# Products q, k, v and of the short convolution: weights as stationary operand, channels on partitions, no VectorE transposes

## The chip, the cores and the metric

The kernel runs on one core of one Trainium2 chip. The metric is the device time of one execution in microseconds (us). The median of three executions of the kernel before is 1896.12 us (1893.32 to 1897.59).

## The reference, cut to what matters

One decoder layer on 256 positions of 2048 channels: two mixers side by side (a gated delta rule, and a short gated convolution), gates, an output projection, and a SwiGLU network. All numbers are float32.

```python
xn = rms_norm(h, ln_mix_g[l])
proj = jnp.einsum('btd,de->bte', xn, w_in[l])
q, k, v, z, b, a, sc_b, sc_c, sc_h, gate_a, gate_b = partition(proj, IN_SIZES)
o_a = gdn_branch(q, k, v, z, b, a, conv_w, ...)   # depthwise conv over time (4 taps), silu,
                                                  # l2 norm of q and k, chunked delta rule
o_b = sc_b * causal_dwconv(sc_c * sc_h, conv_sc_w[l])          # 3 taps
merged = (sigmoid(gate_a) * (o_a @ w_proj_a) + sigmoid(gate_b) * (o_b @ w_proj_b))
h = h + merged @ w_out
hn = rms_norm(h, ln_ffn_g[l])
h = h + (silu(hn @ w_gate) * (hn @ w_up)) @ w_down
return rms_norm(h, ln_final_g)
```

The convolutions run along time, separately for each channel.

## The kernel before, in words

**Tiling.** Every projection is cut into products of 512 output channels. A product contracts 2048 channels in 16 k-tiles of 128 (5632 in 44 for the last one). Weights arrive by DMA in groups of two k-tiles (`raw`, 128x2x512), ScalarE rounds them to a high part (`wh`), VectorE subtracts to get the low part (`wl`), and TensorE makes three matmuls in place of one exact one: high by high, low by high, high by low. The same split of the normed input, with channels on partitions and time along the row, is `xg`; it stays resident for all products from `w_in`.

**Orientation.** In `product` (L383) the 128x128 stationary operand is a piece of the activations (128 channels by 128 positions), and the moving operand is 512 columns of weights. So the result has positions on partitions: two PSUM tiles (m = 0, 1: 128 positions each) of 512 channels, 2 x 3 x 16 = 96 matmuls of 512 columns per product.

**What follows a product.** The normalization factor of a position, `rx`, is a number per partition here, so ScalarE applies it as it moves the PSUM tile out (`evac_rows`, L504). The convolution wants channels on partitions and time along the row, so `flip` (L509) turns the 256x512 block with 16 transposes of 32x256 on VectorE. Then `conv` (L519) runs: ScalarE one tap, VectorE the others. `post_qk` and `post_v` do this for q, k, v of each of four groups of heads; `post_p` and `post_b` for the short convolution: sc_c, its product with sc_h, and sc_b. The products z, of the gates, of the projections and of the feed-forward network stay as they are and are not part of the change.

**Order of products.** Per group g: k, z of the group before, q, v; then four rounds of scc, sch, scb (after the first scc the last z). That is 28 products from the start to 724 us; 24 of them are touched (12 of k, q, v, 12 of scc, sch, scb). Each is 8 groups of weights.

**What sets the order around them.** Each engine runs its instructions in the order in which the program issues them. While `product` issues its matmuls it calls `step` after each k-tile: a planner (`Pace`) keeps an estimated clock per engine, and a follow-up task (a Python generator, one of `post_*`, `decay`, `core`) is advanced when its inputs are estimated to be ready by TensorE's clock. TensorE's small matmuls (the Gram matrices `gr`, sums of squares `ssb`, the triangular inverse `z`, `y`, the outputs `u`, `o`, transposes `vt`, `oc`) are thus dropped in between k-tiles. At most two products may hold PSUM banks (`MM` is 4 banks); before a product starts, `force` advances the most urgent task until one of them is evacuated, ready or not. A ticket (`turn`) lets the follow-ups of k, q, v, scc, scb run one after the other.

**PSUM.** The matmuls of product i+2 go to the banks of product i (in force cases: of product i+1), so they wait for its evacuation.

Of the kernel before, what the change touches and what calls it, by code (L numbers as in the profile page):

```python
# [9 lines left out]
F32 = mybir.dt.float32  # L10
# [5 lines left out]
P = 128  # L16
# [178 lines left out]
def tile_gdn_shortconv_layer(  # L195
# [184 lines left out]
        turn[1] += 1  # L380
        return turn[1] - 1

    def product(stat, KT, nm, after=None, stagger=None, guard=None):  # L383
        while len(pending) > MM // 2 - 1:
            force()
        pt = [ps_mm.tile([P, W], F32, tag="mm", name=f"mm{m}_{nm}") for m in range(2)]

        def terms(m, k, wh, wl):
            hi, lo = stat[k // HG]
            for e, (a, w) in enumerate(((hi, wh), (lo, wh), (hi, wl))):  # L390
                pe.matmul(
                    pt[m], a[:, k % HG, m * P:(m + 1) * P], w[:, k % KGRP, :],
                    start=(k == 0 and e == 0), stop=(k == KT - 1 and e == 2),
                )

        late = KT - KGRP * (AHEAD + 1) if stagger else KT
        kept = []
        for k0 in range(0, KT, KGRP):
            if guard is not None and k0 == KT - HG:
                drain(guard)  # L400
            i = nxt[1]
            nxt[1] += 1
            ensure(i)
            wh, wl = ready.pop(i)
            for k in range(k0, k0 + KGRP):
                for m in range(2):
                    if m == 0 or k < late:
                        terms(m, k, wh, wl)
                    else:
                        kept.append((m, k, wh, wl))  # L410
                if k < k0 + KGRP - 1:
                    step()
            if after is not None:
                after(k0 // KGRP)
            ensure(i + AHEAD + 1)
            step()
        pending.append(pt)
        if kept:
            stagger(pt)
            for t in kept:  # L420
                terms(*t)
        return pt
# [3 lines left out]
    nc.scalar.dma_start(g_mix, ln_mix)  # L426
    ident = gp.tile([P, P], F32, name="ident")
    make_identity(nc, ident)
    ones = gp.tile([P, P], F32, name="ones")
    nc.gpsimd.memset(ones, 1.0)  # L430
    upper = gp.tile([P, P], F32, name="upper")
    lower = gp.tile([P, P], F32, tag="rb", name="lower")
# [39 lines left out]
    def rsqrt(v, n, nm, scale):  # L472
# [17 lines left out]
            dve.scalar_tensor_tensor(out=y, in0=u, scalar=1.5, in1=y, op0=ALU.add, op1=ALU.mult)  # L490
        return y, t

    def bc(ap, n):
        return ap.unsqueeze(2).broadcast_to([P, ap.shape[1], n])

    def rows_tile(nm):
        return io.tile([P, 2, W], F32, tag="rows", name=nm)

    def chan_tile(nm):
        return io.tile([P, HG, T], F32, tag="cv", name=nm)  # L500
# [103 lines left out]
    def scalars():  # L604
# [6 lines left out]
        rx_, _ = rsqrt(ssx, 2, "x", 1.0 / D)  # L611
        dve.tensor_copy(rx, rx_)

    def scalars2():
        yield
        ba = small.tile([P, 2, 2 * H], F32, tag="ba", name="ba", bufs=1)
        bat = gp.tile([2 * H, T], F32, tag="tb", name="bat")
        act.copy(bat, pb[2 * H:])
        dve.tensor_tensor(bat, pb[:2 * H], bat, op=ALU.add)
        for i in range(0, P, SQ):  # L620
            dve.transpose(
                out=ba[i:i + SQ], in_=bat.rearrange("p (m t) -> p m t", t=P)[:, :, i:i + SQ]
            )
        for m in range(2):
            dve.tensor_scalar(
                out=ba[:, m, :], in0=ba[:, m, :], scalar1=rx[:, m:m + 1], scalar2=None, op0=ALU.mult
            )
        sx = small.tile([P, 2, H], F32, tag="spx", name="sp_x", bufs=1)
        dve.tensor_tensor(
            sx, ba[:, :, H:2 * H], dtb.unsqueeze(1).broadcast_to([P, 2, H]), op=ALU.add  # L630
        )
        sa = small.tile([P, 2, H], F32, tag="spa", name="sp_a", bufs=1)
        dve.scalar_tensor_tensor(
            out=sa, in0=sx, scalar=-1.0, in1=sx, op0=ALU.mult, op1=ALU.min
        )
# [14 lines left out]
        yield  # L650
        dve.tensor_copy(gdec_r[:, 0], gdec)
        dve.tensor_tensor(gdec_r[:, 1], gdec, gdec_r[:, 0], op=ALU.subtract)
        dve.tensor_copy(gdec_rf, gdec_r)
        yield 1
        b = bank("aj")
        pe.matmul(b[:, :H], lower, gdec[:, 0, :], start=True, stop=True)
        dve.tensor_copy(aj, b[:, :H])
        mark("gdec")


    def post_qk(g, qk, pt, me):
        while turn[0] < me - 1:
            yield
        nm = f"{'kq'[qk]}{g}"
        rows = rows_tile(f"rows_{nm}")
        evac_rows(pt, rows)
        yield
        if g:
            yield from need(("gram", g - 1))
# [7 lines left out]
        while turn[0] < me:  # L677
            yield
        off = H if qk == 0 else 0
        full = io.tile([P, HG, T], F32, tag="fc", name=f"fc_{nm}", bufs=1)  # L680
        yield from flip(rows, full)
        while turn[0] < me:
            yield
        y = chan_tile(f"cv_{nm}")
        yield from conv(
            full, lambda c, i: wc[:, off + HG * g + c, i:i + 1], 4, y, 0, y
# [47 lines left out]
    def post_v(g, pt, me):  # L734
        while turn[0] < me - 1:
            yield
        nm = f"v{g}"
        rows = rows_tile(f"rows_{nm}")
        evac_rows(pt, rows)
        yield  # L740
        while turn[0] < me:
            yield
        full = io.tile([P, HG, T], F32, tag="fc", name=f"fc_{nm}", bufs=1)
        yield from flip(rows, full)
        while turn[0] < me:
            yield
        y = chan_tile(f"cv_{nm}")
        yield from conv(full, lambda c, i: wc[:, 2 * H + HG * g + c, i:i + 1], 4, y, 0, y)
        turn[0] += 1
        yield  # L750
        yield from need(("sc", g))
        if g:
            yield from need(("done", g - 1))
        yield 2
        vs = st["sc", g][1]
        v = gp.tile([P, 2, HG, P], F32, tag="v", name=f"v_{g}")
        for m in range(2):
            b = bank(f"vt_{g}_{m}")
            for c in range(HG):
                pe.transpose(  # L760
                    b[:, c * P:(c + 1) * P], y[:, c, m * P:(m + 1) * P], ident
                )
            for c in range(HG):
                act.activation(
                    v[:, m, c, :], b[:, c * P:(c + 1) * P], AF.Copy, scale=vs[:, m, c:c + 1]
                )
        mark(("v", g), v)
# [279 lines left out]

    last = None
    for g in range(NG):
        pt = product(xg, KD, f"k{g}", after=None if g else after_first)  # L1050
        if g == 0:
            scalars()
            spawn(scalars2())
        spawn(post_qk(g, 0, pt, ticket()))
        spawn(decay(g))
        last = spawn(core(g))
        if g:
            product_z(g - 1)
        pt = product(xg, KD, f"q{g}")
        spawn(post_qk(g, 1, pt, ticket()))  # L1060
        pt = product(xg, KD, f"v{g}")
        spawn(post_v(g, pt, ticket()))


    ob = [None] * NS

    def post_p(n, pt, me):
        while turn[0] < me - 1:
            yield
        rows = rows_tile(f"scc{n}")  # L1070
        evac_rows(pt, rows)
        yield
        yield from need(("h", n))
        pt = st["h", n]
        for m in range(2):
            dve.scalar_tensor_tensor(
                out=rows[:, m, :], in0=pt[m], scalar=rx[:, m:m + 1], in1=rows[:, m, :],
                op0=ALU.mult, op1=ALU.mult,
            )
        close(pt)  # L1080
        yield
        while turn[0] < me:
            yield
        y = chan_tile(f"sy{n}")
        st["y", n] = y
        ch = io.tile([P, HG, T], F32, tag="fc", name=f"sf{n}", bufs=1)
        yield from flip(rows, ch)
        yield from conv(ch, lambda c, i: wsc[:, HG * n + c, i:i + 1], 3, y, SOON)
        turn[0] += 1

    def post_b(n, pt, me):
        while turn[0] < me - 1:
            yield
        if n == 1:
            yield from need(("oc", NG - 1))
            open_late()
        rows = rows_tile(f"scb{n}")
        evac_rows(pt, rows)
        yield
        while turn[0] < me:  # L1100
            yield
        y = st["y", n]
        ch = io.tile([P, HG, T], F32, tag="fc", name=f"bf{n}", bufs=1)
        yield from flip(rows, ch)
        both(y, y, ch, ALU.mult)
        yield SOON
        if n == 0:
# [10 lines left out]
        ob[1:] = [pair(lp, f"s{NS + i}", f"ob{i}") for i in (1, 2, 3)]  # L1118

    for n in range(NS):  # L1120
        pt = product(xg, KD, f"scc{n}")
        spawn(post_p(n, pt, ticket()))
        if n == 0:
            product_z(NG - 1)
        pt = product(xg, KD, f"sch{n}")
        pace.end = pace.t["pe"]
        mark(("h", n), pt)
        pt = product(xg, KD, f"scb{n}")
        lastb = spawn(post_b(n, pt, ticket()))


# [242 lines left out]
```

## Time and profile before

| | |
|---|---|
| median of 3 runs | 1896.12 us |
| the profiled execution's own time | 1895.74 us |
| its span, first to last instruction | 1893.7 us |
| TensorE busy | 1868.0 us, 99% |
| its weight loads (beside the matmuls) | 1538.5 us, 81% |
| VectorE busy | 1322.7 us, 70% |
| ScalarE busy | 954.0 us, 50% |
| mean granted TensorE clock | 0.996 |

PE is TensorE's matmuls, PEld its weight loads, DVE VectorE, ACT ScalarE. A matmul's duration in the profile (0.39 us for 512 columns) is longer than the distance to the next one's start, since matmuls are pipelined: what a matmul costs in a stream is the distance between starts. The stretch that the change touches ends at 724 us, where the first gate product starts.

### The profile page before, as it was taken

Reading aid. Unit: us, or ns where it says so; the run is one execution under the profiler, and the core shown is the slowest. Engines: PE = TensorE matmul, PEld = TensorE weight load, DVE = VectorE, ACT = ScalarE, POOL = GpSimd, SP = SyncE. Lnnn points to the kernel's source line nnn. Section 1 sums busy time; section 2 is a strip of 40 time slices with the busy share of each in tenths; the row PEclk is TensorE's granted clock in tenths of the full one; section 3 lists DMA queues with packets and bytes.
Section 4 is the critical chain, followed back from the end, with each engine's and each line's share of the span. In section 5 each row is a group of like instructions: output and inputs, shape, how many; then the busy total and the mean of one; then the engine's idle time right before and its main releaser. Section 6 shows DMA issues by size and latency. Waiting matters only on the chain.

```text
span 1893.7 us, 23598 instructions
## 1 busy us (share of the span) xinstructions
PE 1868.0 (99%) x8590; PEld 1538.5 (81%) x8590; DVE 1322.7 (70%) x1923; ACT 954.0 (50%) x1264; POOL 196.3 (10%) x352
## 2 busy tenths in 40 slices
PE   9999999999999999999999999999999999999998
PEld 7888787877887888888888888888888888888886
DVE  6799889688795877444577788666666666644444
ACT  6856866756645545444444444444444444433442
POOL 0006217053171000000000000000000000000000
PEclk9999999999999999999999999999999999999999
DMA  8555546345364566666555565656665555665553
GB/s 308 182 175 192 179 130 205 128 154 179 106 212 152 172 195 212 203 208 199 189 189 189 182 200 185 207 194 196 191 195 194 191 187 190 199 221 189 189 190 133
DMA packets 100356, 354.87 MB, mean 187 GB/s; under 512 B 12176, under 2 KB 12432, under 8 KB 99984
## 3 DMA queue, kind: packets, MB, share of 16 engines
q1 hardware_dynamic: 98432, 349.69, 56.7%
q0 software_dynamic: 1664, 3.67, 0.7%
q8 instruction: 67, 1.10, 0.2%
q14 instruction: 49, 0.40, 0.1%
q10 hardware_dynamic: 144, 0.01, 0.0%
HBM read 350.18 MB, written 3.15 MB: 187 GB/s over the span
## 4 chain that ended last, share of the span: by engine, by line
PE 94%; DVE 3%; ACT 2%; issue 1%; DMA 0%; SPq 0%; DVEq 0%; ACTq 0%
PE mm_dn L170 13%; PE mm_fg L170 13%; PE mm_fu L170 13%; PE mm_proj L170 9%; PE mm_gate L170 9%; PE mm_out L170 5%; PE mm_v L170 4%; PE mm_k L170 4%; PE mm_scb L170 4%; PE mm_z L170 4%; PE mm_scc L170 4%; PE mm_sch L170 4%; PE mm_q L170 4%; DVE wl L189 1%; PE gr L170 1%
## 5 line engine op out<-in xcount | busy, mean ns | idle before, releaser
L189 DVE SCALAR_TENSOR_TENSOR wl<-raw,wh 128x1024 fp32r<-128x1024 f32 (+1 forms) x652 | 793.1, 1226 | 473.6 <-ACT wh L189 468.0
L189 ACT CAST wh<-raw 128x1024 fp32r<-128x1024 f32 (+1 forms) x652 | 681.9, 1047 | 868.2 <-PE mm_fu L170 132.0
L170 PE MATMUL mm_dn<-wh,ff 128*128 128x512 f32 x704 | 219.0, 392 | 0.0
L170 PE MATMUL mm_fg<-wh,hg 128*128 128x512 f32 x704 | 216.7, 389 | 0.0
L170 PE MATMUL mm_fu<-wh,hg 128*128 128x512 f32 x704 | 216.7, 389 | 0.0
L170 PE MATMUL mm_gate<-wh,xg 128*128 128x512 f32 x512 | 157.7, 389 | 0.0
L170 PEld LDWEIGHTS mm_dn<-wh,ff 128*128 128x128 f32 x704 | 132.4, 188 | 29.5
L170 PEld LDWEIGHTS mm_fg<-wh,hg 128*128 128x128 f32 x704 | 132.1, 188 | 27.4
L170 PEld LDWEIGHTS mm_fu<-wh,hg 128*128 128x128 f32 x704 | 132.1, 188 | 27.4
L170 PE MATMUL mm_dn<-wl,ff 128*128 128x512 f32 x352 | 138.0, 392 | 0.0
L170 PE MATMUL mm_fg<-wl,hg 128*128 128x512 f32 x352 | 136.9, 389 | 0.0
L170 PE MATMUL mm_fu<-wl,hg 128*128 128x512 f32 x352 | 136.9, 389 | 0.0
L170 PEld LDWEIGHTS mm_gate<-wh,xg 128*128 128x128 f32 x512 | 96.1, 188 | 20.2
L170 PE MATMUL mm_gate<-wl,xg 128*128 128x512 f32 x256 | 99.7, 389 | 0.0
L170 PE MATMUL mm_sch<-wh,xg 128*128 128x512 f32 x256 | 80.5, 396 | 4.2 <-ACT scc L189 2.7
L170 PE MATMUL mm_q<-wh,xg 128*128 128x512 f32 x256 | 80.7, 396 | 2.4 <-ACT zs L189 1.8
L170 PE MATMUL mm_v<-wh,xg 128*128 128x512 f32 x256 | 80.3, 394 | 0.0
L170 PE MATMUL mm_scb<-wh,xg 128*128 128x512 f32 x256 | 80.1, 394 | 0.0
L170 PE MATMUL mm_out<-wh,m 128*128 128x512 f32 x256 | 80.1, 394 | 0.0
L170 PE MATMUL mm_k<-wh,xg 128*128 128x512 f32 x256 | 79.2, 391 | 0.8 <-ACT wh L189 0.8
L170 PE MATMUL mm_z<-wh,xg 128*128 128x512 f32 x256 | 79.9, 394 | 0.0
L170 PE MATMUL mm_proj<-wh,ob 128*128 128x512 f32 x256 | 79.9, 393 | 0.0
(247 smaller groups left out, 2868.7 us busy)
## 6 DMA issues: line engine op xcount, KB each, us to landing
raw<-in_w_in_dram SPq DMA_DIRECT2D x284, 512.0 KB, 3.5
raw<-in_w_gate_dram SPq DMA_DIRECT2D x88, 512.0 KB, 4.2
raw<-in_w_up_dram SPq DMA_DIRECT2D x88, 512.0 KB, 3.5
raw<-in_w_down_dram SPq DMA_DIRECT2D x88, 512.0 KB, 4.3
raw<-in_w_pb_dram SPq DMA_DIRECT2D x32, 512.0 KB, 3.3
raw<-in_w_pa_dram SPq DMA_DIRECT2D x32, 512.0 KB, 4.2
raw<-in_w_out_dram SPq DMA_DIRECT2D x32, 512.0 KB, 4.2
raw<-in_w_in_dram SPq DMA_DIRECT2D x8, 256.0 KB, 5.9
```

The source lines that it names most:

```text
L170: return f(*a, **k)
L189: return f(*a, **k)
```

## The change

The 24 products of q, k, v, scc, sch, scb are called with `chan=True`. Their matmuls then take 128 columns of the weights as the stationary operand and all 256 positions of `xg` as the moving one. Each of the two PSUM tiles holds two blocks of 128 channels by 256 positions. A product is now 4 x 3 x 16 = 192 matmuls of 256 columns.

The results have channels on partitions already, so `flip` goes away for k, q, v, scc and scb. The factor of a position now lies along the row, so it is spread over all partitions once (`spread`: two small matmuls of ones by a diagonal, then a copy to `rx_row`), and VectorE multiplies by it as it moves a PSUM tile out (`evac_chan`), in place of ScalarE. For the short convolution the squared factor is made once (sc_c by sc_h), and sch multiplies in from PSUM in `evac_chan` as well.

```diff
-    def product(stat, KT, nm, after=None, stagger=None, guard=None):
+    def product(stat, KT, nm, after=None, stagger=None, guard=None, chan=False):
...
             hi, lo = stat[k // HG]
+            if chan:
+                for j in range(2):
+                    cs = slice((2 * m + j) * P, (2 * m + j + 1) * P)
+                    for e, (w, a) in enumerate(((wh, hi), (wh, lo), (wl, hi))):
+
+                        pe.matmul(
+                            pt[m][:, j * T:(j + 1) * T], w[:, k % KGRP, cs], a[:, k % HG, :],
+                            start=(k == 0 and e == 0 and j == 0),
+                            stop=(k == KT - 1 and e == 2 and j == 1),
+                        )
+                return
...
+    def evac_chan(pt, dst, b):
+
+        if len(b.shape) == 2:
+            b = b.unsqueeze(1).broadcast_to([P, HG, T])
+        for m in range(2):
+            cs = slice(2 * m, 2 * m + 2)
+            dve.tensor_tensor(
+                dst[:, cs], pt[m].rearrange("p (c t) -> p c t", t=T), b[:, cs], op=ALU.mult
+            )
+        close(pt)
...
+    def spread():
+        dg = gp.tile([P, 2, P], F32, tag="c32", name="dg")
+        for m in range(2):
+            dve.tensor_scalar(
+                out=dg[:, m, :], in0=ident, scalar1=rx[:, m:m + 1], scalar2=None, op0=ALU.mult
+            )
+        yield 1
+        b = bank("rxb")[:, :T]
+        for m in range(2):
+            pe.matmul(
+                b[:, m * P:(m + 1) * P], ones_r.bitcast(F32), dg[:, m, :], start=True, stop=True
+            )
+        dve.tensor_copy(rx_row, b)
+        mark("rx_row")
...
         nm = f"{'kq'[qk]}{g}"
-        rows = rows_tile(f"rows_{nm}")
-        evac_rows(pt, rows)
+        yield from need("rx_row")
+        full = full_tile(f"full_{nm}")
+        evac_chan(pt, full, rx_row)
...
-        full = io.tile([P, HG, T], F32, tag="fc", name=f"fc_{nm}", bufs=1)
-        yield from flip(rows, full)
-        while turn[0] < me:
-            yield
...
-        pt = product(xg, KD, f"k{g}", after=None if g else after_first)
+        pt = product(xg, KD, f"k{g}", after=None if g else after_first, chan=True)
...
-        rows = rows_tile(f"scc{n}")
-        evac_rows(pt, rows)
+        ch = full_tile(f"scc{n}")
+        if n == 0:
+            st["rx"] = io.tile([P, 2, T], F32, tag="fc", name="rx_rows", bufs=1)
+            dve.tensor_copy(st["rx"][:, 0], rx_row)
+            both(st["rx"][:, 1], rx_row, rx_row, ALU.mult)
+        evac_chan(pt, ch, st["rx"][:, 1])
         yield
         yield from need(("h", n))
-        pt = st["h", n]
-        for m in range(2):
-            dve.scalar_tensor_tensor(
-                out=rows[:, m, :], in0=pt[m], scalar=rx[:, m:m + 1], in1=rows[:, m, :],
-                op0=ALU.mult, op1=ALU.mult,
-            )
-        close(pt)
+        evac_chan(st["h", n], ch, ch)
...
-        ch = io.tile([P, HG, T], F32, tag="fc", name=f"sf{n}", bufs=1)
-        yield from flip(rows, ch)
```

`post_v` and `post_b` change as `post_qk` does, and the calls for q, v, sch and scb as the one for k.

Three places show how instructions move. First TensorE at the head of the first product, before: `mm0`, `mm1` are the two PSUM tiles, `wh0`, `wl0` the first group of weights, `xg0` the input.

```order
L170 MATMUL mm0_k0_212<-wh0_157,xg0_132 128x512 x2
L170 MATMUL mm0_k0_212<-wl0_158,xg0_132 128x512
L170 MATMUL mm1_k0_213<-wh0_157,xg0_132 128x512 x2
L170 MATMUL mm1_k0_213<-wl0_158,xg0_132 128x512
L170 MATMUL mm0_k0_212<-wh0_157,xg0_132 128x512 x2
```

The same place now.

```order
L170 MATMUL mm0_k0_213<-xg0_133,wh0_158 128x256 x2
L170 MATMUL mm0_k0_213<-xg0_133,wl0_159 128x256
L170 MATMUL mm0_k0_213<-xg0_133,wh0_158 128x256 x2
L170 MATMUL mm0_k0_213<-xg0_133,wl0_159 128x256
L170 MATMUL mm1_k0_214<-xg0_133,wh0_158 128x256 x2
L170 MATMUL mm1_k0_214<-xg0_133,wl0_159 128x256
L170 MATMUL mm1_k0_214<-xg0_133,wh0_158 128x256 x2
L170 MATMUL mm1_k0_214<-xg0_133,wl0_159 128x256
```

A k-tile had six matmuls of 512 columns; it has twelve of 256.

Second, TensorE around the sums of squares of k in the last group of heads (`ssb_k3`), before: at the end of product scc0, ahead of z3.

```order
L170 MATMUL mm1_scc0_3893<-wh127_3988,xg3_135 128x512 x2
L170 MATMUL mm1_scc0_3893<-wl127_3989,xg3_135 128x512
L170 MATMUL ssb_k3_4155<-scv_k3_4151,sel_121 32x256 x4
L170 MATMUL ssb_k3_4155<-sfc_k3_4152,sel_121 32x256 x4
L170 MATMUL mm0_z3_4176<-wh128_4075,xg0_132 128x512 x2
L170 MATMUL mm0_z3_4176<-wl128_4076,xg0_132 128x512
```

Now they stand behind the first weight group of product v3.

```order
L170 MATMUL mm1_v3_4754<-xg0_133,wh112_4576 128x256 x2
L170 MATMUL mm1_v3_4754<-xg0_133,wl112_4577 128x256
L170 MATMUL ssb_k3_4789<-scv_k3_4732,sel_121 32x256 x4
L170 MATMUL ssb_k3_4789<-sfc_k3_4733,sel_121 32x256 x4
L170 MATMUL mm0_v3_4753<-xg0_133,wh113_4617 128x256 x2
L170 MATMUL mm0_v3_4753<-xg0_133,wl113_4618 128x256
```

They moved ahead by 15 groups of weights (from behind group 127 to behind group 112), from a place just before a product's start to one inside a product.

Third, the evacuation of scc2, before on ScalarE (product scc2 is the groups 176 to 183; `jk` are squares of the delta rule's output `o`).

```order
L189 CAST wh187_5867<-raw187_5866 128x1024
L189 ACTIVATE jk_3_1_0_5881,so_3_5845<-o1_3_5872,rq_3_4487 128x128
L189 ACTIVATE jk_3_1_1_5883,so_3_5845<-o1_3_5872,rq_3_4487 128x128
L189 ACTIVATE jk_3_1_2_5885,so_3_5845<-o1_3_5872,rq_3_4487 128x128
L189 ACTIVATE jk_3_1_3_5887,so_3_5845<-o1_3_5872,rq_3_4487 128x128
L189 ACTIVATE scc2_5890<-mm0_scc2_5615,rx_131 128x512
L189 ACTIVATE scc2_5890<-mm1_scc2_5616,rx_131 128x512
L189 CAST wh188_5928<-raw188_5927 128x1024
```

Now it is on VectorE.

```order
L189 SCALAR_TENSOR_TENSOR wl185_7454<-raw185_7452,wh185_7453 128x1024
L189 SCALAR_TENSOR_TENSOR wl186_7484<-raw186_7482,wh186_7483 128x1024
L189 TENSOR_TENSOR scc2_7532<-mm0_scc2_7262,rx_rows_5353 128x512
L189 TENSOR_TENSOR scc2_7532<-mm1_scc2_7263,rx_rows_5353 128x512
L189 SCALAR_TENSOR_TENSOR wl187_7514<-raw187_7512,wh187_7513 128x1024
L189 SCALAR_TENSOR_TENSOR wl188_7549<-raw188_7547,wh188_7548 128x1024
```

It stood behind four squares that need the last small matmuls; it stands now between the low parts of two weight groups, and from scc0 on every touched product has its evacuation at this place of its own (behind the low part of group 8(i+1)+2, for product number i counted from 0).

## Rows read from the trace of the kernel before

**Rows 1.** The page, busy time of each engine, share of the span.

```profile
PE 1868.0 (99%) x8590; PEld 1538.5 (81%) x8590; DVE 1322.7 (70%) x1923; ACT 954.0 (50%) x1264; POOL 196.3 (10%) x352
```

**Rows 2.** The page, the chain that ended last, by engine.

```profile
PE 94%; DVE 3%; ACT 2%; issue 1%; DMA 0%; SPq 0%; DVEq 0%; ACTq 0%
```

**Rows 3.** Groups by form, PE: count, busy us, mean ns, idle us before, releasers.

```profile
L170 PE MATMUL mm_q<-wh,xg 128*128 128x512 f32 x256 | 80.7, 396 | 2.4 <-ACT zs L189 1.8 <-ACT rows_k L189 0.6
L170 PE MATMUL mm_sch<-wh,xg 128*128 128x512 f32 x256 | 80.5, 396 | 4.2 <-ACT scc L189 2.7 <-ACT zs L189 1.5
...
L170 PE MATMUL u<-v,R 128*128 128x128 f32 x64 | 8.4, 275 | 0.0
...
L170 PE MATMUL vt<-ident,cv_v 128*128 128x128 f32 x32 | 4.6, 276 | 2.5 <-DVE ua L189 2.5
...
L170 PE MATMUL ssb_k<-sfc_k,sel 128*32 128x256 f32 x16 | 2.9, 313 | 0.3 <-DVE sfc_k L189 0.3
L170 PE MATMUL ssb_k<-scv_k,sel 128*32 128x256 f32 x16 | 2.9, 313 | 4.3 <-ACT scv_k L189 4.3
```

**Rows 4.** Stretches: us, busy PE, PEld, DVE, ACT, POOL, granted clock, DMA, GB/s.

```profile
0.00:724.00 724.00, 707.42 (x3503) 582.92 (x3504) 592.84 (x1032) 450.13 (x732) 196.34 (x352) 0.99 0.55 179
...
419.90:424.60 4.70, 4.35 (x15) 3.10 (x14) 3.45 (x9) 0.53 (x1) 3.92 (x11) 0.51 0.00 0
...
612.50:615.60 3.10, 3.08 (x7) 2.48 (x8) 2.69 (x16) 0.55 (x1) 0.32 (x1) 0.50 0.22 83
```

**Rows 5.** Timeline, PE, first product: start us, duration us, form.

```profile
23.51 1.33 PE L170 MATMUL pba<-xg,wbs 128*64 128x256 f32 x10
24.68 0.62 PE L170 MATMUL mm_k<-wh,xg 128*128 128x512 f32 x2
...
27.41 0.86 PE L170 MATMUL pba<-xg,wbs 128*64 128x256 f32 x6
```

**Rows 6.** Timeline, PE, six matmuls of the Gram matrices.

```profile
135.25 0.28 PE L170 MATMUL gr<-kh 128*128 128x256 f32 x1
135.36 0.28 PE L170 MATMUL gr<-kh,kl 128*128 128x256 f32 x1
...
135.82 0.28 PE L170 MATMUL gr<-kl,kh 128*128 128x256 f32 x1
135.94 0.40 PE L170 MATMUL mm_q<-wh,xg 128*128 128x512 f32 x1
```

**Rows 7.** Timeline, PEld, the weight loads of these.

```profile
135.25 0.19 PEld L170 LDWEIGHTS gr<-kh,kl 128*128 128x128 f32 x1
135.37 0.19 PEld L170 LDWEIGHTS gr<-kl,kh 128*128 128x128 f32 x1
```

**Rows 8.** Groups by form, DVE and ACT.

```profile
L189 DVE STREAM_TRANSPOSE fc_q<-rows_q 32x256 f32<-32x256 f32 x64 | 27.9, 436 | 1.1
...
L189 DVE SCALAR_TENSOR_TENSOR scc<-mm_sch,rx,scc 128x512 f32<-128x512 f32 x8 | 5.6, 745 | 0.0
L189 DVE TENSOR_TENSOR zs<-o,zs 128x512 f32<-128x512 f32 x8 | 5.5, 690 | 16.3 <-ACT jk L189 16.3
...
L189 ACT ACTIVATE rows_k<-mm_k,rx 128x512 f32<-128x512 f32 x8 | 5.0, 677 | 0.9 <-DVE rx L189 0.9
```

**Rows 9.** Timeline, PE, around three waits.

```profile
326.90 0.39 PE L170 MATMUL mm_z<-wl,xg 128*128 128x512 f32 x1
329.06 0.73 PE L170 MATMUL mm_q<-wh,xg 128*128 128x512 f32 x2 [1.77 <-ACT zs L189]
...
421.58 1.05 PE L170 MATMUL mm_z<-wh,xg 128*128 128x512 f32 x2
...
424.79 0.39 PE L170 MATMUL mm_z<-wl,xg 128*128 128x512 f32 x1
...
612.52 1.22 PE L170 MATMUL mm_sch<-wh,xg 128*128 128x512 f32 x2 [2.66 <-ACT scc L189]
...
615.92 0.40 PE L170 MATMUL mm_sch<-wl,xg 128*128 128x512 f32 x1
```

More of the change, by code (lines that the diff above doesn't have):

```diff
@@ L428, in tile_gdn_shortconv_layer @@
     make_identity(nc, ident)
-    ones = gp.tile([P, P], F32, name="ones")
+    ones = gp.tile([P, P], F32, tag="c32", name="ones")
     nc.gpsimd.memset(ones, 1.0)
@@ L491, in rsqrt @@
         return y, t
+    rx_row = gp.tile([P, T], F32, name="rx_row")
+    def evac_chan(pt, dst, b):
[7 more added lines that the diff above has]
+        close(pt)
     def bc(ap, n):
@@ L497, in rows_tile, with full_tile @@
         return io.tile([P, 2, W], F32, tag="rows", name=nm)
+    def full_tile(nm):
+        return io.tile([P, HG, T], F32, tag="rows", name=nm)
     def chan_tile(nm):
@@ L737, in post_v @@
         nm = f"v{g}"
-        rows = rows_tile(f"rows_{nm}")
-        evac_rows(pt, rows)
+        yield from need("rx_row")
+        full = full_tile(f"full_{nm}")
+        evac_chan(pt, full, rx_row)
         yield
[L741 to L744, printed above, removed]
         while turn[0] < me:
@@ L1049, in tile_gdn_shortconv_layer @@
     for g in range(NG):
-        pt = product(xg, KD, f"k{g}", after=None if g else after_first)
+        pt = product(xg, KD, f"k{g}", after=None if g else after_first, chan=True)
         if g == 0:
             scalars()
+            spawn(spread())
             spawn(scalars2())
@@ L1058, in tile_gdn_shortconv_layer @@
             product_z(g - 1)
-        pt = product(xg, KD, f"q{g}")
+        pt = product(xg, KD, f"q{g}", chan=True)
         spawn(post_qk(g, 1, pt, ticket()))
-        pt = product(xg, KD, f"v{g}")
+        pt = product(xg, KD, f"v{g}", chan=True)
         spawn(post_v(g, pt, ticket()))
@@ L1069, in post_p @@
             yield
-        rows = rows_tile(f"scc{n}")
-        evac_rows(pt, rows)
+        ch = full_tile(f"scc{n}")
[4 more added lines that the diff above has]
+        evac_chan(pt, ch, st["rx"][:, 1])
         yield
         yield from need(("h", n))
-        pt = st["h", n]
-        for m in range(2):
-            dve.scalar_tensor_tensor(
-                out=rows[:, m, :], in0=pt[m], scalar=rx[:, m:m + 1], in1=rows[:, m, :],
-                op0=ALU.mult, op1=ALU.mult,
-            )
-        close(pt)
+        evac_chan(st["h", n], ch, ch)
         yield
@@ L1096, in post_b @@
             open_late()
-        rows = rows_tile(f"scb{n}")
-        evac_rows(pt, rows)
+        ch = full_tile(f"scb{n}")
+        evac_chan(pt, ch, st["rx"][:, 0])
         yield
@@ L1102, in post_b @@
         y = st["y", n]
-        ch = io.tile([P, HG, T], F32, tag="fc", name=f"bf{n}", bufs=1)
-        yield from flip(rows, ch)
         both(y, y, ch, ALU.mult)
@@ L1120, in tile_gdn_shortconv_layer @@
     for n in range(NS):
-        pt = product(xg, KD, f"scc{n}")
+        pt = product(xg, KD, f"scc{n}", chan=True)
         spawn(post_p(n, pt, ticket()))
@@ L1124, in tile_gdn_shortconv_layer @@
             product_z(NG - 1)
-        pt = product(xg, KD, f"sch{n}")
+        pt = product(xg, KD, f"sch{n}", chan=True)
         pace.end = pace.t["pe"]
         mark(("h", n), pt)
-        pt = product(xg, KD, f"scb{n}")
+        pt = product(xg, KD, f"scb{n}", chan=True)
         lastb = spawn(post_b(n, pt, ticket()))
```

## The prediction

> **What bounds the kernel now.** I read the busy times first. TensorE is busy 99% of the span, VectorE 70%, ScalarE 50% [rows 1]; the chain that ended last is 94% TensorE, 3% VectorE [rows 2]. So relieving VectorE is worth nothing by itself, and two questions are left. What does TensorE's own work cost in its new shape? And how much of TensorE's idle time was made by the work that goes away? For the first I need distances between matmul starts, so I read the timeline where 512 and 256 columns stand side by side [rows 5, 6]. For the second I read the groups of TensorE by form with the idle time before them and who ended it [rows 3], and then the places themselves [rows 9]. The touched stretch is 0 to 724 us: VectorE is at 592.8 of 724 us (82%) there, ScalarE at 450.1 (62%), TensorE at 707.4 [rows 4].
>
> **Part 1: the matmuls.** Removed are 24 products x 96 = 2304 matmuls of 512 columns, added 24 x 192 = 4608 of 256. The columns that stream through are the same (1,179,648); the count of matmuls and of weight loads doubles. In the first product 12 matmuls of 512 start between 24.68 and 27.41 us: 2.73 / 12 = 227.5 ns each [rows 5]. 2304 x 227.5 ns = 524.2 us, waits not counted.
>
> For 256 columns there are two kinds of rows. Ten `pba` matmuls, whose moving operand is the very `xg` of the change but with a stationary operand of 64 columns, take 23.51 to 24.68: 117.0 ns each [rows 5]. Six `gr` matmuls with a full 128x128 stationary operand, a new one each time, take 135.25 to 135.94: 115 ns each [rows 6]. The trace has no run of 256 columns longer than these. Bounds: a gain in streaming is excluded, since the columns are the same, so the low end is half of 227.5, 113.75 ns, or 524.2 us: no loss. The high end is the longest single distance in the six, 135.82 to 135.94 [rows 6], 120 ns, or 553.0 us: a loss of 28.8. I take 115.5, nearer to the `gr` rows because they alone load 128 columns of weights for each matmul, and a little above them because the `pba` rows are the longer run: 4608 x 115.5 = 532.2 us. **Term 1: +8.0 us.**
>
> Is the doubled number of weight loads hidden? A load of 128x128 lasts 0.19 us and the next starts 0.12 us later, while the matmul before it (0.28 us from 135.25) is still running: loads overlap matmuls and each other [rows 6, 7]. The Trainium skill speaks against this: "TensorE: Matmul & The Clock Gate", Part 3, "The mechanism", says in its list of what overlaps that a weight load runs beside a matmul only when the row groups differ, and here all loads use all 128 rows. By that rule 2304 more loads of 0.19 us would be bare, +438 us; the trace disagrees with it, and in this kernel's rows the load is hidden.
>
> **Part 2: TensorE's waits that belong to the old evacuation.** Idle before mm_q is 2.4 us, before mm_sch 4.2, before ssb_k 4.3 and 0.3 [rows 3]: 11.2 us. All of them sit where a product was about to start while the PSUM tile of an earlier one still waited in ScalarE's queue, or where a follow-up had been forced before its inputs were there; the third place in the order shows scc2 behind four squares of `o`, the second ssb_k3 at a product's edge. Each wait costs a refill on top: from 326.90 to 329.06 is 2.16 us, less one distance of 0.23 leaves 1.93, against 1.77 us shown as idle [rows 9]. With some six such places that is 1.0 us. After the two longest the granted clock is 0.51 and 0.50 for a while, the 1.2 GHz level, after 4.3 and 2.7 us of idle [rows 3, 4]: eight matmuls take 421.58 to 424.79 = 3.21 us in place of 1.82, and 612.52 to 615.92 = 3.40 [rows 9]. That is 3.0 us. Sum 15.2 us.
>
> Why should they go? Each flip is 16 transposes of 436 ns, 7.0 us, and 20 products lose one: 139.5 us off VectorE. The added evacuations are 48 of about 0.69 us, 33.1, less the 8 multiplications of sch that they replace (0.745 each, 6.0). VectorE loses 112 us net; with 480 of 724 us (66%) the planner has no backlog there, and ScalarE loses 40 evacuations of 0.68 us, 27 us [rows 4, 8]. In the new order every evacuation from scc0 on stands right behind the end of its product, a whole product (22 us) before its banks are wanted. **Term 2: -15.2 us.** Its bounds: 0 if other waits of the same size take their place; -17.7 if the 2.5 us before `vt`, which ended on VectorE [rows 3], go too.
>
> The evacuation is a new wait for VectorE: it waits for the last matmul of its product. Behind it on VectorE stands the low part of the group of weights that TensorE wants three groups later, 24 new-size matmuls each or 3 x 2.77 = 8.3 us; the two evacuation instructions are 1.4 us, the low part 1.2. So TensorE is not made to wait by it. SP's order of DMA issues is the same, and no queue is passed.
>
> **Part 3: spreading the factor.** Two matmuls of 128 columns in plain float32, which show as two each (the code's 32 `u` matmuls are 64 rows [rows 3]); at the price of a 256-column one each, 4 x 0.117 = 0.5 us. The diagonal, the copy and the squared factor lie on VectorE beside k0 and q0. Nothing waits for `rx_row` before v0 wants k0's banks. **Term 3: +0.5 us.** Between 0, if it falls into another wait, and 3, if TensorE stands before the diagonal as long as it did before mm_sch.
>
> **Sum.** 8.0 - 15.2 + 0.5 = -6.7 us. The profiled execution took 1895.74 (span 1893.7 and 2.0 around it); the median of the runs is 0.4 above it. 1895.7 - 6.7 + 0.4 = 1889.4 us.
>
> **Rivals.** (a) The 256-column stream settles slower, at 119 ns, the upper part of the bounds. For it: no long run exists, `pba` is already at 117.0, and the load of 0.19 us has less matmul to hide behind. Against it: the six `gr` rows at full weights. Then term 1 is 4608 x 119 = 548.4, +24.2, and the sum +9.5: 1905.6 us, slower. It decides from (524.2 + 14.7) / 4608 = 117.0 ns on, which is exactly the `pba` row: the margin is thin.
> (b) The waits are not removed but moved: the planner packs the chain of a head group tighter, and TensorE stands before `y`, `u` or `vt` in place of mm_q and mm_sch. For it: `vt` already waits 2.5 us on VectorE [rows 3]. Against: 112 us less VectorE work. With half of term 2 left the sum is +0.9: 1897.0 us, no change.
> (c) A 256-column matmul costs just half a 512-column one: term 1 is 0, the sum -14.7: 1881.4 us. For it: the starts inside the six go down to 0.11 us apart [rows 6]. Against: ten `pba` in a row do not get there.
> (d) Weight loads are not hidden in a long stream: +438 us, some 2320. Six loads in a row speak against it.
>
> **Chances.** A measurement of this kernel can tell about 0.2%, 3.8 us, from no change. Forecast 0.46, with a range of its own from 1883 to 1895; (a) 0.20, (b) 0.19, (c) 0.13, (d) 0.02. Most of the forecast's share and all of (c) are faster: 0.52. Slower are (a), (d) and a little of (b): 0.25. The rest, 0.23, is within 0.2%. The range from 1879 (term 1 at its low end, `vt` gone too) to 1908 (119.5 ns, with term 2 whole) leaves out about 2 in 10.
>
> **What would show it.** In the profile after, the distance between starts in a touched product's stream says at once which of forecast, (a) and (c) holds: 115.5, 119 or 113.75 ns. Idle time before mm_q and mm_sch should be near 0, ssb_k's below 1 us, and no stretch from 20 to 724 us should show a granted clock of 0.5. VectorE's busy time should fall by about 110 us, ScalarE's by 27, and the first gate product should start at about 717 us in place of 724. I am wrong if VectorE's relief shows and the gate product starts no earlier: then either the stream is at 117 ns or more, or the waits have moved.

## The result: slower by 0.6%, and the profile after

The changed kernel takes 1907.53 us (median of 4 runs, 1906.42 to 1907.66) against 1895.0 for the kernel before (4 runs): a ratio of 1.0063 with an interval of [1.005, 1.0076], or 12.5 us slower. 1889.4 were forecast. The profiled execution took 1907.52 us, with a span of 1905.8.

The page after: busy time of each engine, and the chain that ended last.

```profile
PE 1892.5 (99%) x10898; PEld 1660.7 (87%) x10898; DVE 1215.8 (64%) x1648; ACT 925.1 (49%) x1220; POOL 200.9 (11%) x352
...
PE 92%; issue 3%; POOL 2%; ACT 1%; DMA 1%; DVE 0%; SPq 0%; POOLq 0%; DVEq 0%; ACTq 0%
```

Against [rows 1, 2] VectorE lost 106.9 us (forecast 112) and ScalarE 28.9 (forecast 27). VectorE is gone from the chain, where GpSimd now stands with 2%. TensorE has 2308 matmuls more and is busy for 24.5 us more. So the relief came as computed, and the kernel is slower all the same: TensorE's own work grew by more than its waits shrank.

Where on the time axis? The first gate product marks the end of the touched stretch. The view of the tile `mm_gate`: minimum, median and maximum duration, first and last start. Before:

```profile
L170 PE MATMUL mm_gate<-wh,xg x512: 387/389/397, 723.9 to 1051.8; 128*128 128x512 f32 x171
```

After:

```profile
L170 PE MATMUL mm_gate<-wh,xg x512: 387/389/397, 736.0 to 1063.9; 128*128 128x512 f32 x171
```

It starts 12.1 us later and then runs as before; from there to the end of the span both have 1169.8 us. The whole loss lies ahead of it. The stretch up to it, to be read against the first row of [rows 4] (same columns):

```profile
0.00:736.00 736.00, 731.84 (x5810) 705.01 (x5811) 491.70 (x772) 422.28 (x689) 200.93 (x352) 1.00 0.56 177
```

TensorE is not busy for 4.2 us of it, where it was 16.6 us before, and the mean granted clock rounds to 1.00. The waits did go, but for one that is new and is shown below. What came in their place is in the timeline of TensorE, in the middle of a touched product (start, duration, form):

```profile
300.04 0.40 PE L170 MATMUL mm_k<-xg,wh 128*128 128x256 f32 x2
...
301.84 0.40 PE L170 MATMUL mm_k<-xg,wh 128*128 128x256 f32 x2
```

Fifteen matmuls start in 1.80 us, 120.0 ns each. This is the very number that the profile was to give for the forecast (115.5) or rival (a) (119), and it is the upper end of my bounds. The weight loads under it, in the timeline of PEld:

```profile
300.17 0.19 PEld L170 LDWEIGHTS mm_k<-xg,wl 128*128 128x128 f32 x1
300.29 0.31 PEld L170 LDWEIGHTS mm_k<-xg,wh 128*128 128x128 f32 x2
```

A load lasts 0.19 us, the next one starts 0.12 us later: they overlap each other and the matmuls, as in [rows 7]. Rival (d) is out.

The groups of TensorE by form, for [rows 3]:

```profile
L170 PE MATMUL mm_q<-xg,wh 128*128 128x256 f32 x512 | 92.8, 283 | 0.0
...
L170 PE MATMUL mm_sch<-xg,wh 128*128 128x256 f32 x512 | 93.3, 284 | 0.0
...
L170 PE MATMUL oc<-ident,zs 128*128 128x128 f32 x32 | 5.3, 279 | 2.0 <-POOL zs L189 1.9
...
L170 PE MATMUL vt<-ident,cv_v 128*128 128x128 f32 x32 | 4.1, 272 | 0.0
...
L170 PE MATMUL ssb_k<-scv_k,sel 128*32 128x256 f32 x16 | 2.5, 279 | 0.0
...
L170 PE MATMUL rxb<-dg,ones_r 128*128 128x128 f32 x4 | 0.6, 273 | 0.0
```

The 2.4, 4.2, 4.3 and 2.5 us before mm_q, mm_sch, ssb_k and vt are all 0.0. One new wait of 2.0 us stands before `oc`. In the timeline of TensorE (in brackets the idle time and what ended it):

```profile
586.27 0.33 PE L170 MATMUL oc<-ident,zs 128*128 128x128 f32 x1 [0.24 <-POOL zs L189]
588.25 0.55 PE L170 MATMUL oc<-ident,zs 128*128 128x128 f32 x3 [1.65 <-POOL zs L189]
```

And GpSimd just before:

```profile
584.27 3.93 POOL L189 TENSOR_TENSOR zs<-zs,rsy_o 128x512 f32<-128x512 f32 x2 [40.46 <-DVE rsy_o L189]
```

GpSimd needs 3.93 us for two multiplications, and TensorE reaches the first `oc` less than 2 us after they began. In the kernel before, `oc` started 5.7 us after them (620.96 against 615.28 us). This is rival (b) in small: one wait of 2 us came where 11.2 went. The clock fell behind it. The windows view just after, columns as above:

```profile
589.00:592.50 3.50, 3.50 (x19) 3.50 (x18) 1.82 (x2) 1.47 (x2) 0.00 (x0) 0.51 0.47 146
```

For 3.5 us the granted clock is 0.51, the 1.2 GHz level, though the prediction had said that no stretch from 20 to 724 us would show a granted clock of 0.5. The seventeen matmuls that start from 589.00 us on take 3.52 us there in place of 2.04: 1.5 us lost on top of the wait.

### The profile page after: what moved, and what is told of

It reads as the page before. It is cut to its first block, busy times and chain, and to the rows that moved or that the text cites. A ratio compares the mean times of both kernels' runs of the same rounds, so it can differ in the third digit from the quotient of the medians.

```text
span 1905.8 us, 27885 instructions
## 1 busy us (share of the span) xinstructions
PE 1892.5 (99%) x10898; PEld 1660.7 (87%) x10898; DVE 1215.8 (64%) x1648; ACT 925.1 (49%) x1220; POOL 200.9 (11%) x352
## 3 DMA queue, kind: packets, MB, share of 16 engines
q8 instruction: 85, 1.39, 0.3%
## 4 chain that ended last, share of the span: by engine, by line
PE 92%; issue 3%; POOL 2%; ACT 1%; DMA 1%; DVE 0%; SPq 0%; POOLq 0%; DVEq 0%; ACTq 0%
PE mm_dn L170 13%; PE mm_fg L170 13%; PE mm_fu L170 13%; PE mm_proj L170 9%; PE mm_gate L170 9%; PE mm_v L170 5%; PE mm_q L170 5%; PE mm_out L170 5%; PE mm_k L170 5%; PE mm_z L170 4%; PE mm_scc L170 4%; PE mm_sch L170 4%; PE mm_scb L170 3%; POOL tb L189 1%; POOL rb L189 1%
## 5 line engine op out<-in xcount | busy, mean ns | idle before, releaser
L170 PE MATMUL mm_scb<-xg,wh 128*128 128x256 f32 x512 | 94.8, 287 | 0.0
L170 PE MATMUL mm_sch<-xg,wh 128*128 128x256 f32 x512 | 93.3, 284 | 0.0
L170 PE MATMUL mm_k<-xg,wh 128*128 128x256 f32 x512 | 92.8, 283 | 0.0
L170 PE MATMUL mm_q<-xg,wh 128*128 128x256 f32 x512 | 92.8, 283 | 0.0
L170 PE MATMUL mm_v<-xg,wh 128*128 128x256 f32 x512 | 92.6, 283 | 0.0
L170 PE MATMUL mm_scc<-xg,wh 128*128 128x256 f32 x512 | 92.3, 283 | 0.0
L170 PEld LDWEIGHTS mm_scb<-xg,wh 128*128 128x128 f32 x512 | 80.7, 194 | 0.1
```

Of the source, the lines that this page charges most:

```text
L170: return f(*a, **k)
```

## The experiments

Theory 1 is that a 256-column matmul behind a 128-column weight load costs 120 ns whatever stands still, so that the doubled count is the loss. Its rival is the orientation: weights as stationary operand, read along another stride, cost more. Behind theory 1 stand three readings of why it is 120 and not 113.75: a fixed price per load (1a), the length of a load (1b), a rate of issue (1c). The second theory is that the flips and ScalarE's evacuation made the waits. Wherever a ratio is given, the kernel before was timed on the same chip.

**e1_halves** leaves everything of the kernel before as it is, and only cuts the matmuls of the 24 products in two.

```diff
+SHAPE = {nm: (P, (256, 256)) for nm in ("k", "q", "v", "scc", "sch", "scb")}
...
-                pe.matmul(
-                    pt[m], a[:, k % HG, m * P:(m + 1) * P], w[:, k % KGRP, :],
-                    start=(k == 0 and e == 0), stop=(k == KT - 1 and e == 2),
-                )
+                for r in range(0, P, rows):
+                    c = 0
+                    for n in cuts:
+                        pe.matmul(
+                            pt[m][r:r + rows, c:c + n], a[:, k % HG, m * P + r:m * P + r + rows],
+                            w[:, k % KGRP, c:c + n],
...
```

Expected: 

> The kernel before (activations stationary, ScalarE evacuation, transposes), but each 512-column matmul of the 24 products is cut into two of 256 columns with the same stationary operand. Theory 1 (any 256-column matmul with a 128x128 weight load settles at 120 ns in a long stream, whichever operand is stationary): 4608 x 120.0 - 524.2 = +28.8 us, the waits of before stay, about 1924 us, and the starts stand 120 ns apart. Rival 2 (the price comes from the new orientation: freshly written weights as stationary operand): starts 114 to 116 ns apart as in the six Gram matmuls, +1 to +10 us, 1896 to 1905 us.

Measured: 1921.34 us, ratio 1.0139 [1.0122, 1.0156]. Timeline of TensorE in a cut product:

```profile
299.86 0.64 PE L171 MATMUL mm_k<-wh,xg 128*128 128x256 f32 x4
...
302.50 0.40 PE L171 MATMUL mm_k<-wl,xg 128*128 128x256 f32 x2
```

22 matmuls in 2.64 us: 120.0 ns, with the activations standing still. So it is the number of columns behind a load, not which operand is loaded; the orientation is refuted. The page counts 10894 weight loads, one for each matmul, where the kernel before has 8590: the second half has its stationary operand loaded again, although it is the same. Groups by form, and the tile `mm_gate`, of the same kernel:

```profile
L171 PE MATMUL mm_sch<-wh,xg 128*128 128x256 f32 x512 | 83.9, 287 | 4.2 <-ACT scc L190 2.7 <-ACT zs L190 1.5
L171 PE MATMUL mm_q<-wh,xg 128*128 128x256 f32 x512 | 83.6, 285 | 2.4 <-ACT zs L190 1.8 <-ACT rows_k L190 0.6
...
L171 PE MATMUL ssb_k<-scv_k,sel 128*32 128x256 f32 x16 | 3.0, 313 | 3.1 <-ACT scv_k L190 3.1
```

```profile
L171 PE MATMUL mm_gate<-wh,xg x512: 387/389/397, 749.6 to 1077.5; 128*128 128x512 f32 x171
```

The waits stand nearly as before, and the gate product starts 25.7 us late. That is the price of the cut alone, with the little that the waits shrank by already taken off.

**e5_noflip** takes the flips out of the kernel before: the rows are read as if they held channels already, so the output is not the reference's.

```diff
-        full = io.tile([P, HG, T], F32, tag="fc", name=f"fc_{nm}", bufs=1)
-        yield from flip(rows, full)
+        full = rows.rearrange("p m w -> p (m w)").rearrange("p (c t) -> p c t", t=T)
+        yield SOON
```

The same edit stands in `post_v` and in the two places of the short convolution. Expected: 

> The kernel before with its 512-column matmuls and ScalarE evacuation, but without the 16 transposes of each of the 20 flips: the convolutions read the rows as they lie, so the result is not the reference's. If the waits of before were made by the transposes' time on VectorE (the second term of the prediction): about 15 to 17 us less than before, 1878 to 1880 us, no idle before mm_q, mm_sch and ssb_k. Rival (they came from ScalarE's evacuation, which stays here): less than 5 us gained.

Measured: 1876.21 us, ratio 0.9901 [0.9887, 0.9916]: 19.1 us faster. Groups by form and the tile `mm_gate`:

```profile
L170 PE MATMUL mm_sch<-wh,xg 128*128 128x512 f32 x256 | 79.6, 392 | 0.0
L170 PE MATMUL mm_q<-wh,xg 128*128 128x512 f32 x256 | 79.0, 390 | 0.0
...
L170 PE MATMUL oc<-ident,zs 128*128 128x128 f32 x32 | 5.3, 278 | 1.2 <-POOL zs L189 1.2
```

```profile
L170 PE MATMUL mm_gate<-wh,xg x512: 387/389/397, 705.3 to 1033.2; 128*128 128x512 f32 x171
```

The gate product starts 18.6 us earlier. ScalarE still evacuates here, so its place in the evacuation was not what mattered: the waits named after ScalarE's `zs` and `scc` [rows 3] were the flips' doing, further up.

**e4_shapes** gives each of the six kinds of product another shape, to see the distance between starts as a function of loaded and streamed columns. Where fewer columns are loaded, both halves of a block are added into the same rows of PSUM, so the output is not the reference's, and the whole time (2291.27 us) says nothing.

```diff
+SHAPE = {
+    "k": (P, (128,) * 4), "q": (64, (256, 256)), "v": (64, (512,)),
+    "scc": (P, (384, 128)), "sch": (64, (128,) * 4), "scb": (P, (320, 192)),
+}
```

Expected: 

> The kernel before, in which the matmuls of six products are cut in other ways, to read the distance between starts in long streams (stationary columns x moving columns): k 128x128, q 64x256, v 64x512, scc 128x384 and 128x128 in turn, sch 64x128, scb 128x320 and 128x192 in turn. In the 64-column pieces of q, v, sch the second half is added to the first half's rows, so the result is not the reference's; the time of the whole says nothing. Theory 1a (a fixed part of 13.3 ns on top of columns / 2.4 GHz, whatever the load): 128 columns 66.7, 192 93.3, 320 146.7, 384 173.3, 512 226.7 ns. Theory 1b (bound by the weight load, start to start at least 112 to 120 ns for 128 stationary columns): 128x128 and 128x192 at 112 to 120 ns, 64x256 below 117, 64x128 below 70. Theory 1c (bound by the issue of two instructions per matmul): every shape up to 256 columns at 120 ns.

Timeline of TensorE in the middle of four kinds of product (stationary rows and columns, then moving):

```profile
201.81 1.06 PE L174 MATMUL mm_k<-wh,xg 128*128 128x128 f32 x8
...
204.04 0.61 PE L174 MATMUL mm_k<-wl,xg 128*128 128x128 f32 x4
...
260.10 0.62 PE L174 MATMUL mm_q<-wl,xg 128*64 128x256 f32 x4
...
261.92 0.96 PE L174 MATMUL mm_q<-wh,xg 128*64 128x256 f32 x7
...
840.21 0.45 PE L174 MATMUL mm_scc<-wl,xg 128*128 128x384 f32 x2
...
842.79 0.39 PE L174 MATMUL mm_scc<-wl,xg 128*128 128x384 f32 x1
...
879.81 1.00 PE L174 MATMUL mm_sch<-wh,xg 128*64 128x128 f32 x14
...
881.13 0.58 PE L174 MATMUL mm_sch<-wh,xg 128*64 128x128 f32 x7
```

128 columns behind 128 loaded ones: 20 matmuls in 2.23 us, 111.5 ns. 256 behind 64: 16 in 1.82, 113.8. 128 behind 64: 22 in 1.32, 60.0. The pair 384 + 128, both behind 128 loaded columns: 18 matmuls in 2.58 us, 143.3 each, 287 the pair.

A fixed price per load (1a) falls: 128 moving columns at half of 113.75 plus 6.25 would be 63, not 111.5, and 256 behind 64 pay nothing. A rate of issue (1c) falls with the 60.0. At 128 moving columns the distance follows the loaded ones, 111.5 for 128 and 60.0 for 64; at 128 loaded columns, halving the moving ones takes 120.0 only to 111.5. So the loads bound short matmuls (1b): not by the 0.19 us that one of them lasts, but by how closely one follows the other. The cut at 384 + 128 shows it in a sum: 287 is near to 111.5 for the short part and 170.6 (three quarters of 227.5) for the long one, 282.

**e7_loads** asks what is left of the 120: does the extra appear only where load and stream are equally long? Again only the distances count, part of each product is left out, and the whole time (1950.24 us) says nothing.

```diff
+SHAPE = {
+    "k": (96, (256, 256)), "q": (112, (256, 256)), "v": (120, (256, 256)),
+    "scc": (P, (272, 240)), "sch": (32, (256, 256)), "scb": (96, (128,) * 4),
+}
```

Expected: 

> The kernel before in which six products use other shapes (stationary columns x moving columns), to read the distance between starts: k 96x256, q 112x256, v 120x256, scc 128x272 and 128x240 in turn, sch 32x256, scb 96x128. Only the first rows of each block are computed with the narrower stationary operands, so the result is not the reference's. Theory (a matmul costs the longer of its stream, columns / 2.26, and its load, 112 ns for 128 columns, and some 7 ns more only where the two are nearly equal): 96x256 and 32x256 at 113.4 ns, 112x256 near 113.4, 120x256 between 113.4 and 120, the pair 272 + 240 at 232 to 238 ns in place of 240, 96x128 at 84 to 88 ns. Rival (the extra over 113.3 grows steadily with the stationary columns): 96x256 near 116, 112x256 near 118, 120x256 near 119.

Timeline of TensorE, two of the kinds:

```profile
464.85 0.40 PE L174 MATMUL mm_sch<-wl,xg 128*32 128x256 f32 x2
...
467.67 0.40 PE L174 MATMUL mm_sch<-wl,xg 128*32 128x256 f32 x2
...
709.85 0.40 PE L174 MATMUL mm_scc<-wl,xg 128*128 128x272 f32 x2
...
712.69 0.28 PE L174 MATMUL mm_scc<-wl,xg 128*128 128x272 f32 x1
```

256 columns behind only 32 loaded ones: 24 in 2.82 us, 117.5 ns, no better than the 117.0 of the 64-column `pba` rows [rows 5]. The pair 272 + 240: 24 in 2.84, 118.3, so 237 for 512 columns. 96, 112 and 120 loaded columns mostly gave 116 to 118 as well. But 112 loaded columns hold two paces in one run:

```profile
35.66 0.62 PE L174 MATMUL mm_q<-wh,xg 128*112 128x256 f32 x4
...
39.06 0.62 PE L174 MATMUL mm_q<-wh,xg 128*112 128x256 f32 x4
...
146.17 0.40 PE L174 MATMUL mm_q<-wl,xg 128*112 128x256 f32 x2
...
148.99 0.28 PE L174 MATMUL mm_q<-wl,xg 128*112 128x256 f32 x1
```

Thirty matmuls start in 3.40 us at first, 113.3 ns each, and 24 in 2.82 us later, 117.5 ns. The theory falls in part: 128 loaded columns are the worst case, but shorter loads mostly cost some 3 to 4 ns too, and that part is not set by the shape alone, since one shape shows it and does not. What sets it, and why 64 loaded columns reached 113.8 in e4 and 32 did not here, stays open.

**e2_qkv** does the change for q, k and v alone, 12 of the 24 products.

```diff
+def CHAN(nm):
+    return not nm.startswith("sc")
...
-        pt = product(xg, KD, f"k{g}", after=None if g else after_first)
+        pt = product(xg, KD, f"k{g}", after=None if g else after_first, chan=CHAN(f"k{g}"))
```

Where `CHAN` says no, the old path stands. To make room for both paths, this kernel and the next three also hold some small tiles in one buffer in place of two; no run tells what that alone does to the time. Expected: 

> The change for q, k, v alone; scc, sch, scb as before with ScalarE evacuation and transposes. If the two terms add up product by product: 12 products x 192 x 120.8 ns less 12 x 96 x 227.5 ns = +16.2 us, and the waits, which all hang on the delta rule's follow-ups, go as with the whole change, -16 us: 1895 us, same as before. If the gain needs all flips gone: 1903 to 1911 us.

Measured: 1891.27 us, ratio 0.9981 [0.9971, 0.999]: 4.1 us faster than before, where no difference was expected. Groups by form:

```profile
L174 PE MATMUL mm_sch<-wh,xg 128*128 128x512 f32 x256 | 79.5, 392 | 0.0
```

The wait before mm_sch is gone although the short convolution is untouched: twelve of the twenty flips off VectorE are enough.

**e3_sc** does the other half alone (`nm.startswith("sc")`); the squared factor is applied in two steps here. Expected: 

> The change for scc, sch, scb alone (the factor applied to scc twice in place of its square once); q, k, v with ScalarE evacuation and transposes. Cost as for the other half: 12 x 1.35 = +16.2 us. The flips of q, k, v stay, and with them their late evacuations; if the waits belong to the backlog of q, k, v, only those before sch2 (2.7 us idle, 1.6 us of clock) go: -4 to -6 us, so 1904 to 1908 us. If any half of the VectorE work would do: 1893 to 1896.

Measured: 1911.19 us, ratio 1.0083 [1.0068, 1.0099], above what I expected. Groups by form:

```profile
L174 PE MATMUL mm_sch<-xg,wh 128*128 128x256 f32 x512 | 94.1, 286 | 5.7 <-DVE scc L193 4.2 <-ACT zs L193 1.5
...
L174 PE MATMUL mm_q<-wh,xg 128*128 128x512 f32 x256 | 80.7, 397 | 2.4 <-ACT zs L193 1.8 <-ACT rows_k L193 0.6
```

The flips of q, k and v stay, and the waits with them. The evacuation of scc is VectorE's now, and TensorE stands 4.2 us before mm_sch where ScalarE had made it stand 2.7. VectorE's timeline shows what is ahead of that evacuation, which starts at 619.69 us:

```profile
615.38 0.69 DVE L193 TENSOR_TENSOR zs<-o,zs 128x512 f32<-128x512 f32 x1 [1.39 <-ACT jk L193]
```

VectorE stood idle for 1.39 us there, and for 4.84 us before the half ahead of it, for ScalarE's squares `jk`; then a chain of small instructions on `o` and a low part follow, and only then the evacuation. So VectorE is not full at this place but behind in order. The forecast's claim that VectorE reaches an evacuation at once does not hold with these flips left in; the whole change, without them, has no wait before mm_sch.

**e6_q** does the change for the four q alone (`nm[0] == "q"`), the least that might cure the waits. Expected: 

> The change for the four q products alone. Cost 4 x 1.35 = +5.4 us. In the order all evacuations but those of v0 and scb1 stand right behind their products; if the backlog of k and q behind each other makes the waits, most of the 19 us that the kernel without transposes gained come: -12 to -17 us, so 1883 to 1888 us, faster than both kernels. If each wait needs its own flip gone: 1896 to 1899 us.

Measured: 1890.01 us, ratio 0.9973 [0.9961, 0.9984], 5.9 us faster, but short of what I expected. Groups by form:

```profile
L174 PE MATMUL mm_sch<-wh,xg 128*128 128x512 f32 x256 | 80.6, 396 | 1.3 <-ACT scc L193 1.3
...
L174 PE MATMUL oc<-ident,zs 128*128 128x128 f32 x32 | 5.5, 287 | 3.6 <-POOL zs L193 3.6
...
L174 PE MATMUL vt<-ident,cv_v 128*128 128x128 f32 x32 | 4.4, 274 | 1.0 <-DVE ua L193 1.0
```

In these three groups 5.9 us of waits are still there. The profiled execution took 1892.37 us, 2.4 above the median, so the median one may have fewer.

**e8_kq** does it for k and q (`nm[0] in "kq"`), eight products. Expected: 

> The change for the k and q products alone (8 of 24). Cost 8 x 1.35 = +10.8 us, waits gone as in the variant with q, k, v: -16 to -20 us, so 1886 to 1891 us; slower than the variant with q alone if that one already loses its waits.

Measured: 1889.87 us, ratio 0.9966 [0.9954, 0.9979], as expected. Groups by form:

```profile
L174 PE MATMUL mm_sch<-wh,xg 128*128 128x512 f32 x256 | 79.6, 392 | 0.0
```

e2, e6 and e8 beat the kernel before by 4 to 6 us of 1895, and their medians lie 16 to 18 us below that of the whole change; between e6 and e8 no difference can be told.

The five partial changes side by side. Paid is 96 x (2 x 120.0 - 227.5) = 1.2 us for each changed product; won is the measured difference less that.

| changed | products | paid | measured | won by waits |
|---|---|---|---|---|
| q | 4 | +4.8 | -5.9 | -10.7 |
| k, q | 8 | +9.6 | -6.0 | -15.6 |
| q, k, v | 12 | +14.4 | -4.1 | -18.5 |
| scc, sch, scb | 12 | +14.4 | +15.3 | +0.9 |
| all | 24 | +28.8 | +12.5 | -16.3 |

The price grows with every product, while the waits are worth some 16 to 19 us in all and four products earn more than half of that. It matters which flips go, more than how many: e3 and e8 both take eight off, and e3 wins next to nothing. With e1's measured difference as the price (26.0 us for 24 products) the last column reads, row by row, -10.2, -14.7, -17.1, +2.3 and -13.5.

The clock follows the waits. Between its first rise and the gate product, the traces' records of the granted clock have stretches at half clock of 10.2 us in all in the kernel before, in e1 and in e3, of 6.8 in e6, of 3.4 in e8 and in the whole change, and none in e2 and e5.

## Why the prediction was wrong

**The step that failed** is in part 1: "I take 115.5, nearer to the `gr` rows because they alone load 128 columns of weights for each matmul". Term 1 measures 4608 x 120.0 = 553.0 us, +28.8 in place of +8.0, which is the upper end of its bounds. The mechanism was named right (rival (a)), and the size was off by 20.8 us, more than the whole forecast gain. The six `gr` rows have the shape of the products' matmuls, but not their price. Of the six, the first distance reads 0.11 us and the last one 0.12 [rows 6]; the last one, my upper bound, is what e1 and the changed kernel hold for whole products. e1 shows that the price does not come from which operand is loaded. Nor were the six cheap for standing behind 512-column matmuls: in the changed kernel six `gr` matmuls stand inside a stream of 256 columns, behind twelve of its matmuls:

```profile
246.13 0.28 PE L170 MATMUL gr<-kh,kl 128*128 128x256 f32 x1
...
246.59 0.28 PE L170 MATMUL gr<-kl,kh 128*128 128x256 f32 x1
```

These four distances are 0.46 us, 115 ns each, as before. So I took the mean of one stream for the price of another. What makes the `gr` rows cheaper stays open: their moving operand is two pieces of 128 columns, where the products have one of 256, but no run separates that.

**Bounds.** The lower one was drawn from the columns alone; the 113.8 of e4 behind 64 loaded columns comes to it, so it was a true bound, but not for a load of 128. A bound from the loads was missing, although the trace of the kernel before had it, in the outputs `o` of the delta rule:

```profile
248.95 1.95 PE L170 MATMUL o<-u,ua 128*128 128x128 f32 x16
```

Less the 0.28 us of the last one, fifteen distances take 1.67 us: 111 ns for 128 columns behind 128 loaded ones, and e4 gives 111.5. Stream and load are thus almost equally long at 256 columns. Neither bound gives the 120.0: it lies above both, and e7 leaves open where the part that shorter loads pay as well comes from. (The trace before also had twelve `pba` rows in a stretch, at 31.31 us and again 117 ns, a longer run than the prediction says.) The Trainium skill ("TensorE: Matmul & The Clock Gate", section "LDWEIGHTS (loading the stationary operand)") prices a load by its columns; its formula gives an estimate of 107 ns for 128, and e4's 111.5 and 60.0 bear out that columns set it. The Trainium skill, same title, section "Back-to-back issue gap", says that spacing is set by load and matmul together, which the trace bears out; its isolated gap for 256 columns is 262 cycles, an estimate of 109 ns by its figures, where the trace has 120.0, and the measurement decides.

**Loads hidden:** right, 120 ns a matmul under loads of 190. The overlap rule of the Trainium skill that the prediction weighed ("TensorE: Matmul & The Clock Gate", Part 3, "The mechanism"), which lets a load run beside a matmul only when the row groups differ, does not hold in these rows.

**Term 2, -15.2:** right in kind, and if anything too small. By difference the changed kernel has 12.1 - 28.8 - 0.5 = -17.2, near the bound of -17.7: `vt` went as well. e5, which removes only the flips, has -18.6 at the gate product. The idle time fell by 12.4 us with the new wait already counted in. Of the half-clock part most went, but not all: the two stretches of before [rows 4] are gone, and one of 3.4 us came behind the new wait. That ScalarE's evacuation had to go too was an unneeded part of the reasoning: e5 keeps it. The wait before `oc` (2.0 us) and the 1.5 us of clock behind it are the share that came back.

The pieces do not quite add: 25.7 (e1) - 18.6 (e5) + 0.5 = 7.6 us, against 12.1. Of the 4.5 left, 1.9 are waits that e1's longer products already cover (ssb_k 4.3 to 3.1, vt 2.5 to 2.0, mm_k 0.8 to 0.6) and that e5 counts again, and 0.8 is the longer wait before `oc`. Of the other 1.8, the half-clock stretch behind that wait is 1.5, which neither e5, with no such stretch, nor the difference of e1 has. 0.3 us stay unexplained.

**Term 3, +0.5:** 4 matmuls, 0.6 us of busy time with no idle time before them; right.

**Rivals.** (a), 119 ns on from a threshold of 117.0, came true at 120.0; its 1905.6 us is 1.9 below the median. Its evidence was the `pba` row itself, which stood on that threshold. Its other reason, that the load has less matmul to hide behind, is at most a part: 32 loaded columns give 117.5 in e7. (b) is the 2.0 us before `oc` with 1.5 of clock, (c) and (d) are out.

## What to carry to other kernels

Swapping operands keeps the streamed columns but changes how often weights are loaded: halving the moving width from 512 to 256 columns cost 12.5 ns for each pair here, and it is paid on every matmul that is cut. Take the price of a matmul from a long run of the same stream: six matmuls of the same shape kept 115 ns inside a stream of 120, so the shape alone does not give it. Where the trace has only a handful, the upper bound deserves more than the chance of a tail. And where a change buys off waits by relieving another engine, do it for the few parts that the waits hang on: a third of this change (k and q) won 15.6 of the waits' 16 to 19 us, and the rest mostly paid.

## What the runs showed of the hardware

At 512 columns behind 128 loaded ones the distance is 227.5 ns, behind 64 (v in e4) it is 230: a shorter load buys nothing there. A strongly uneven cut costs more than an even one: 512 columns in 256 + 256 take 240 ns, in 272 + 240 some 237, in 320 + 192 (scb in e4) 259, in 384 + 128 287; the short part is held to the length of a load while the long one is not shortened.

The first 82 us of e4 seem not to fit their own granted clock. TensorE's timeline, the same shape twice:

```profile
24.15 1.91 PE L174 MATMUL mm_k<-wh,xg 128*128 128x128 f32 x8
...
83.54 1.06 PE L174 MATMUL mm_k<-wh,xg 128*128 128x128 f32 x8
```

And the windows view of the first 60 us (columns as in [rows 4]):

```profile
6.40:67.00 60.60, 60.60 (x285) 60.60 (x286) 17.90 (x31) 17.01 (x29) 0.00 (x0) 1.00 0.46 169
```

The starts are 213 ns apart at first, nearly double the later 111.5, while the view reads 1.00. But the trace's record of the granted clock begins only at 82.45 us of this run, with full clock (at 5.4 us in the changed kernel), and the view counts a time without a record as full. The distances change in just this place, and at the recorded 0.51 of the changed kernel the distance is 213 to 214 ns too. So the first 82 us of e4 ran at the 1.2 GHz level, although TensorE was busy without a gap from 6.4 us on; what let the clock rise then, no run shows.
